# One weight tile of a mixture-of-experts layer moved into the memory of x and of work space: a blind prediction on one Trainium2 core

## The chip, the cores and the metric

One NeuronCore of one Trainium2 chip runs the whole program. Its engines are named as the profile names them: PE (TensorE, the matrix engine), PEld (its weight load), DVE (VectorE), ACT (ScalarE), POOL (GpSimd) and SP (SyncE, which issues nearly all transfers here; SPq is its queue). The metric is the device time of one execution in microseconds (us); less is better.

## The reference

Two transformer blocks follow each other on 256 tokens of width 1024, all in float32. The first is attention with eight heads, a layer norm and a mixture of experts; the second is a recurrent mixer with a short convolution, and a gated feed-forward net. What takes most of the time is the mixture of experts: 32 experts, each token goes to the four with the highest router logits.

```python
logits = (xt @ w_router + b_router)
top_logit, top_e = lax.top_k(logits, TOP_K)        # TOP_K = 4 of 32 experts
gate = jax.nn.softmax(top_logit, axis=-1)
...
h = xb @ w_gu[e] + b_gu[e]                          # [rows, 1024] @ [1024, 2048]
h_gate, h_up = jnp.split(h, 2, axis=-1)
h_gate = jnp.minimum(h_gate, SWIGLU_LIMIT)
h_up = jnp.clip(h_up, -SWIGLU_LIMIT, SWIGLU_LIMIT)
act = h_gate * jax.nn.sigmoid(SWIGLU_ALPHA * h_gate) * (h_up + 1.0)
return act @ w_down[e] + b_down[e]                  # [rows, 1024] @ [1024, 1024]
...
y = jax.ops.segment_sum(y_assign * gate, tok_sorted)
h = layer_norm(DEEPNORM_ALPHA * h + f, ln_g[i, 1], ln_b[i, 1])
```

## The kernel before

**Weight tiles.** All 32 experts are computed, so all their weights come in from HBM: per expert four gate and up tiles and two down tiles of 2 MB each (16 KB on each of 128 partitions). They are called gu*e*.*c* (c from 0 to 3) and dn*e*.*c* (c 0 or 1) in this text. The list `loads` holds them in the order of transfer: gu0.0 to gu0.3, gu1.0 to gu1.3, dn0.0, dn0.1, gu2.0 to gu2.3, dn1.0, dn1.1, gu3.0 and so on. Each is one `dma_start` on SP's queue (`load_run`, L125).

**Ten places.** During the mixture of experts a tile lies in one of ten places that are taken in rotation: six of the pool `wa`, open from the start, and four of the pool `wb` (`IN_B`), which is opened once the attention's memory is free. `weight(key, AHEAD)` asks for a tile and has `pump` queue the loads up to nine tiles further on; the load of the tile that is ten later in the list needs the place of the tile just used, so SP waits there until PE has read it. gu2.0 follows into the place of gu0.0, gu3.2 into that of dn0.0, dn2.0 into that of gu2.0.

**Order of the work.** For each expert `gate_up(e)` (L779, with the bias at L785) multiplies the gathered token rows by the four gate and up tiles, `swiglu` (L760 to L764) makes the activation on DVE and ACT, `transpose_act` (L794) turns it, and one expert later `finish(e - 1)` runs `down` (L807), `down_out` (L816) and, for odd experts, `combine` (L830, L831) into `y`. Two experts share one gathered batch: `make_batch` (L683) gathers it, `weigh_batch` (L748 to L755) prepares its weights. `y` is the memory of `xtok`, which held x for the attention. `start_y` fills `y`: eight multiplications and additions of rows on DVE (L655, L657) with the rows broadcast by PE (L259) through the two banks "m" of PSUM, a transpose and its copy `GT` (L661, L662), and four products with the down biases `bdn` (L667, L668). It is called after `gate_up(0)`. `bdn`, the output piece `ys`, the gate piece `sw_g` and the activation `at` are tiles of the pool `p2`; `bdn` and `ys` share a tag, each tag has one buffer.

Outside the stretches that are marked as ordered by hand, the framework orders the instructions of each engine itself when the program is built: among those that are ready by its own reckoning, the one that comes first in the program. After expert 15 a branch (`overflow`, L836) covers experts with more than 64 rows; here it is not taken.

Of the kernel before, what the change touches and what calls it, by code (L numbers as in the profile page):

```python
# [22 lines left out]
P = 128  # L23
# [60 lines left out]
def block_kernel(ctx: ExitStack, tc: tile.TileContext, a: dict, out: bass.AP, dbg=None):  # L84
# [37 lines left out]
    def load_run(t, w, r0, n):  # L122
# [3 lines left out]
                          .rearrange("(p k) c -> p (k c)", k=n))  # L126

    def load_run_last(t, w, r0, n):

        cols = w.shape[1]  # L130
        v = t[:, 0:n * cols].rearrange("p (k c) -> p k c", c=cols)
        for k, m in ((0, 2), (2, 1), (3, 1)):
            nc.sync.dma_start(v[:, k:k + m], w[r0:r0 + n * P, :]
                              .rearrange("(p k) c -> p k c", k=n)[:, k:k + m])
# [26 lines left out]
    for e in range(NE + 1):  # L161
        gu = [(("gu", e, c), load_run, (w_gu[e], c * 256, 2)) for c in range(4) if e < NE]
        dn = [(("dn", e - 1, c), load_run, (w_dn[e - 1], c * 512, 4)) for c in range(2) if e > 0]
        loads += dn + gu if e == OVF_AT else gu + dn
    end_moe = len(loads)
    loads[-1] = (loads[-1][0], load_run_last, loads[-1][2])
# [17 lines left out]
    def pump(upto):  # L184
        while state["next"] < min(upto, len(loads)):
            i = state["next"]
            key, fn, args = loads[i]
            slot = (i - first_moe) % (SLOTS_A + len(IN_B))
            if first_moe <= i < end_moe and slot in IN_B:
                if "b" not in pools:  # L190
# [8 lines left out]
    def weight(key, ahead=SLOTS_A - 1):  # L199
        pump(order[key] + 1 + ahead)  # L200
        return tiles.pop(key)
# [402 lines left out]
    with ExitStack() as c2:  # L604
# [6 lines left out]

        bdn = p2.tile([NE, D], F32, name="bdn", tag="ys")
        nc.gpsimd.dma_start(bdn, a["moe_b_down"][0])

# [143 lines left out]
        def swiglu(dst, pg, pu):  # L758
            gt = p2.tile([P, 512], F32, name="sw_g", tag="sw_g")
            V.tensor_scalar(gt, pg, LIMIT, None, op0=OP.min)  # L760
# [5 lines left out]
        def gate_up(e):  # L766
# [5 lines left out]
            for c in range(4):  # L772
                w = weight(("gu", e, c), AHEAD).rearrange("p (k c) -> p k c", c=2 * FF)
                for k in range(2):
                    kt = 2 * c + k
                    for q, dst in ((0, pg), (1, pu)):
                        for h in range(2):
                            c0 = q * FF + h * 512
                            mm(dst[h * CAP:(h + 1) * CAP, :], xs[:, kt, col:col + CAP],  # L779
                               w[:, k, c0:c0 + 512], start=(kt == 0), stop=(kt == KT - 1))  # L780
                if c == 0:
                    for q, dst in ((0, pg), (1, pu)):
                        for h in range(2):
                            c0 = q * FF + h * 512
                            mm(dst[h * CAP:(h + 1) * CAP, :], sel_e, bgu[:, c0:c0 + 512],  # L785
                               start=False, stop=False)
            at = p2.tile([P, 512], F32, name="at", tag="act")
            swiglu(at, pg, pu)
            return at

        def transpose_act(at, tag="aT", copy=nc.any.tensor_copy):
            pt = bank("atp", [P, 4, P], "t")
            for j in range(4):
                nc.tensor.transpose(pt[:, j, :], at[:, j::4], ident)  # L794
            aT = p2.tile([P, 4, P], F32, name="aT", tag=tag)
            copy(aT, pt)  # L796
# [13 lines left out]
        def down_out(e, pd):  # L810
            if e % 2 == 0:
                ys_pair[e // 2] = p2.tile([P, 2, 512], F32, name="ys", tag="ys")
            ys = ys_pair[e // 2]
# [19 lines left out]
        def overflow():  # L833

            n = nc.values_load(cnti[0:1, 0:1], min_val=0, max_val=NE)
            with tc.If(n > 0), tc.For_i(0, n, 1) as e:  # L836
                for g in range(2):
# [31 lines left out]
                    for kt in range(KT):  # L869
                        for q in range(2):  # L870
                            w = p2.tile([P, FF], F32, name="ow", tag="ys")
                            nc.sync.dma_start(
# [6 lines left out]
                    for h in range(2):  # L879
                        at = p2.tile([P, 512], F32, name="oat", tag="act")  # L880
                        swiglu(at, acc[0][h], acc[1][h])
# [3 lines left out]
                    for kt in range(KT):  # L885
                        w = p2.tile([P, D], F32, name="owd", tag="ys")
                        nc.sync.dma_start(w, w_dn[bass.ds(e, 1), kt // 4 * 512 + kt % 4:kt // 4 * 512 + 512:4, :]
# [55 lines left out]
        for e in range(NE):  # L943
# [11 lines left out]
            if e == NE - 1:  # L955
# [5 lines left out]
                break  # L961
            if e == 0:
                start_y()
            if e % NB == NB - 1 and e + 1 < NE and e + 1 != OVF_AT:
# [492 lines left out]
```

## Time and profile before

| | |
|---|---|
| Median of three runs | 1403.62 us (1400.08 to 1406.6) |
| The profiled execution | 1397.48 us |
| Its span, first to last instruction | 1395.7 us |
| PE busy | 1319.1 us, 95% |
| Read from HBM | 476.70 MB, 342 GB/s over the span |
| Granted clock of PE, mean | 0.991 |

The profiled execution is 1.78 us longer than its span and 6.1 us shorter than the median of the runs. A busy PE in this table is one with a matmul in its pipeline; the stretches below show which of PE and the transfers waits for the other.

### The profile page before, as it was taken

To read this page: it belongs to the slowest core of one execution; us is meant where nothing else is said; L and a number is where in the kernel's file an instruction comes from. 1 tells how busy PE (TensorE), PEld (TensorE's weight loads), DVE (VectorE), ACT (ScalarE), POOL (GpSimd) and SP (SyncE) were. 2 spreads that over 40 slices of the span, in tenths; PEclk is the share of its full clock that TensorE was granted. 3 is DMA by queue.
4 is the path that set the end of the run, shared out by engine and by line. 5 is a ranking of instruction groups with operands and counts; after the bars stand their busy time and mean duration, and the time that the engine had idled before them with its cause. 6 is when DMAs were issued, how large, how long until landed. Compare 5 with 4: busy or idle time off the path is not lost.

```text
span 1395.7 us, 16947 instructions
## 1 busy us (share of the span) xinstructions
PE 1319.1 (95%) x7162; PEld 749.0 (54%) x7162; DVE 527.6 (38%) x925; ACT 324.8 (23%) x571; POOL 73.2 (5%) x47
## 2 busy tenths in 40 slices
PE   9999999999999998798988989999899999999998
PEld 8887334334333332343433323333235998899997
DVE  4675322222222112221221212212115686777776
ACT  4553010011011000000001000000114445655554
POOL 2520000000000000000000000000003321000000
PEclk9999999999999999999999999999999999999999
DMA  8977999999999999989999999999999424555500
GB/s 260 356 284 295 381 426 427 427 426 427 428 426 426 427 427 427 424 350 428 427 428 425 428 426 426 427 427 428 427 421 387 148 81 161 184 199 190 182 1 31
DMA packets 74948, 478.91 MB, mean 343 GB/s; under 512 B 4764, under 2 KB 31972, under 8 KB 50196
## 3 DMA queue, kind: packets, MB, share of 16 engines
q1 hardware_dynamic: 74756, 477.61, 84.1%
q8 instruction: 58, 0.95, 0.3%
q0 software_dynamic: 112, 0.17, 0.0%
q14 instruction: 22, 0.18, 0.0%
HBM read 476.70 MB, written 1.06 MB: 342 GB/s over the span
## 4 chain that ended last, share of the span: by engine, by line
PE 30%; DMA 25%; DVE 2%; ACT 0%; issue 0%; SPq 0%; DVEq 0%; ACTq 0%
PE pu L266 9%; DMA wb<-in_moe_w_gate_up_dram 8%; DMA w<-in_moe_w_gate_up_dram 8%; DMA wb<-in_moe_w_down_dram 6%; PE pq L266 4%; DMA w<-in_moe_w_down_dram 3%; PE pg L779 2%; PE pu L779 2%; PE pd L807 2%; PE fa L270 1%; PE fa L272 1%; PE fa L271 1%; PE pgat L683 1%; PE px L1224 1%; PE pc L830 1%; PE mo L272 1%
## 5 line engine op out<-in xcount | busy, mean ns | idle before, releaser
L779 PE MATMUL pg<-w,xs 128*64 128x512 f32 x616 | 177.2, 599 | 12.5 <-DMA w<-in_moe_w_gate_up_dram 12.5
L779 PE MATMUL pu<-w,xs 128*64 128x512 f32 x616 | 178.2, 592 | 0.0
L760 DVE TENSOR_SCALAR sw_g<-pg 128x512 f32<-128x512 f32 x32 | 22.1, 691 | 401.4 <-PE pg L779 401.4
L807 PE MATMUL pd<-w,aT 128*64 128x512 f32 x624 | 142.6, 596 | 16.3 <-DMA w<-in_moe_w_down_dram 15.7
L761 ACT ACTIVATE at<-sw_g 128x512 f32<-128x512 f32 x32 | 20.2, 630 | 552.1 <-DVE sw_g L760 552.1
L779 PE MATMUL pg<-wb,xs 128*64 128x512 f32 x408 | 112.1, 602 | 10.0 <-DMA wb<-in_moe_w_gate_up_dram 10.0
L779 PE MATMUL pu<-wb,xs 128*64 128x512 f32 x408 | 110.9, 597 | 0.0
L807 PEld LDWEIGHTS pd<-w,aT 128*64 128x64 f32 x624 | 44.9, 137 | 102.2 <-issue 76.2
L993 ACT CAST hi<-w 128x1024 fp32r<-128x1024 f32 x75 | 78.4, 1048 | 86.3 <-PE pu L266 39.4
L779 PEld LDWEIGHTS pu<-w,xs 128*64 128x64 f32 x616 | 51.3, 137 | 86.7 <-issue 86.4
L779 PEld LDWEIGHTS pg<-w,xs 128*64 128x64 f32 x616 | 46.8, 136 | 94.8 <-issue 85.3
L807 PE MATMUL pd<-wb,aT 128*64 128x512 f32 x400 | 92.6, 606 | 4.9 <-DMA wb<-in_moe_w_down_dram 4.9
L816 DVE COPY ys<-pd 64x512 f32<-64x512 f32 x32 | 21.9, 684 | 187.4 <-PE pd L807 187.4
L994 DVE TENSOR_TENSOR lo<-w,hi 128x1024 fp32r<-128x1024 f32 x60 | 74.0, 1234 | 43.1 <-ACT hi L993 40.4
L994 POOL TENSOR_TENSOR lo<-w,hi 128x1024 fp32r<-128x1024 f32 x15 | 36.0, 2406 | 1005.7 <-DVE st L1091 938.6
L683 PEld LDWEIGHTS pgat<-oh,h 128*128 128x128 f32 x512 | 66.8, 208 | 23.5 <-issue 21.9
L683 PE MATMUL pgat<-oh,h 128*128 128x128 f32 x512 | 72.1, 299 | 6.8 <-DVE oh L677 6.4
L796 ACT COPY aT<-atp 128x512 f32<-128x512 f32 x32 | 18.7, 585 | 228.2 <-PE pd L807 183.3
L779 PEld LDWEIGHTS pu<-wb,xs 128*64 128x64 f32 x408 | 31.6, 138 | 58.1 <-issue 58.1
L779 PEld LDWEIGHTS pg<-wb,xs 128*64 128x64 f32 x408 | 29.3, 137 | 62.4 <-issue 54.4
L830 PE MATMUL pc<-ys,wT 128*128 128x512 f32 x120 | 57.2, 609 | 2.4 <-DVE ys L816 2.4
L807 PEld LDWEIGHTS pd<-wb,aT 128*64 128x64 f32 x400 | 27.6, 138 | 56.5 <-issue 47.7
(321 smaller groups left out, 1865.6 us busy)
## 6 DMA issues: line engine op xcount, KB each, us to landing
w<-in_moe_w_gate_up_dram SPq DMA_DIRECT2D x77, 2048.0 KB
wb<-in_moe_w_gate_up_dram SPq DMA_DIRECT2D x51, 2048.0 KB
w<-in_moe_w_down_dram SPq DMA_DIRECT2D x38, 2048.0 KB
wb<-in_moe_w_down_dram SPq DMA_DIRECT2D x25, 2048.0 KB
w<-in_ffn_w_up_dram SPq DMA_DIRECT2D x22, 1024.0 KB
w<-in_w_in_dram SPq DMA_DIRECT2D x6, 2048.0 KB
w<-in_a_w_in_dram SPq DMA_DIRECT2D x5, 2048.0 KB
w<-in_ffn_w_down_dram SPq DMA_DIRECT2D x5, 2048.0 KB
```

What stands on the lines that cost most here:

```text
L266: mm(psum_ap, lhs[:, kt, :], rhs[:, kt, :], start=(i == 0 and kt == kts[0]), stop=(i == len(pairs) - 1 and kt == kts[-1]))
L272: mm(psum_ap, ll, rh, start=False, stop=last)
L683: mm(pg[:, j, :], h1[:, tt, chan(kt)], batches[b][1][:, tt].rearrange("p e s -> p (e s)"), start=start, stop=stop)
L760: V.tensor_scalar(gt, pg, LIMIT, None, op0=OP.min)
L761: act(dst, gt, AF.Sigmoid, scale=SW_ALPHA)
L779: mm(dst[h * CAP:(h + 1) * CAP, :], xs[:, kt, col:col + CAP], w[:, k, c0:c0 + 512], start=(kt == 0), stop=(kt == KT - 1))
L796: copy(aT, pt)
L807: mm(pd[h][h * CAP:(h + 1) * CAP, :], lhs, w[:, k, h * 512:(h + 1) * 512], start=(c == 0 and k == 0), stop=(c == 1 and k == 3))
L816: (nc.scalar.copy if h else V.tensor_copy)(ys[o:o + CAP, h, :], pd[h][h * CAP:(h + 1) * CAP, :])
L830: mm(pc, lhs[:, tt * P:(tt + 1) * P], ys[:, h, :], start=True, stop=True)
L993: nc.scalar.copy(hi, piece)
L994: (nc.gpsimd if on_pool else V).tensor_sub(lo, piece, f32(hi))
```

## The change

gu0.3, the fourth tile that the first expert needs, is taken out of its place in `loads` and put behind gu2.0 as the eleventh load. It gets a place of its own that is used once: its rows with k = 0 go to the memory of `xtok`, those with k = 1 to a new tile `late` of 8 KB a partition in `p2`, by two transfers of 1 MB (`load_run_rows`). The other tiles keep the rotation of ten, from which gu0.3 is left out: gu1.0 takes the place that gu0.3 had, every tile up to gu2.0 moves up by one, gu2.1 follows into the place of gu0.0, and from dn1.0 on each load follows into the place of the same tile as before. `late` later serves as `sw_g`, `at` and `ys`, and as `bdn`; so `bdn` is loaded after `gate_up(0)` and `start_y` is called after `gate_up(1)`, as `y` is the memory of `xtok`.

```diff
@@ -125,6 +125,12 @@
         nc.sync.dma_start(t[:, 0:n * cols], w[r0:r0 + n * P, :]
                           .rearrange("(p k) c -> p (k c)", k=n))
 
+    def load_run_rows(t, w, r0, n):
+
+        for k in range(n):
+            nc.sync.dma_start(t[k], w[r0:r0 + n * P, :]
+                              .rearrange("(p k) c -> p k c", k=n)[:, k])
+
     def load_run_last(t, w, r0, n):
 
         cols = w.shape[1]
@@ -162,6 +168,10 @@
         gu = [(("gu", e, c), load_run, (w_gu[e], c * 256, 2)) for c in range(4) if e < NE]
         dn = [(("dn", e - 1, c), load_run, (w_dn[e - 1], c * 512, 4)) for c in range(2) if e > 0]
         loads += dn + gu if e == OVF_AT else gu + dn
+
+    ONCE = first_moe + SLOTS_A + len(IN_B)
+    key, _, args = loads.pop(first_moe + 3)
+    loads.insert(ONCE, (key, load_run_rows, args))
     end_moe = len(loads)
     loads[-1] = (loads[-1][0], load_run_last, loads[-1][2])
     W2_ORDER = (2, 1, 0, 3, 5, 6, 4)
@@ -185,8 +195,12 @@
         while state["next"] < min(upto, len(loads)):
             i = state["next"]
             key, fn, args = loads[i]
-            slot = (i - first_moe) % (SLOTS_A + len(IN_B))
-            if first_moe <= i < end_moe and slot in IN_B:
+            slot = (i - first_moe - (i > ONCE)) % (SLOTS_A + len(IN_B))
+            if i == ONCE:
+                if "once" not in pools:
+                    return
+                t = pools["once"]
+            elif first_moe <= i < end_moe and slot in IN_B:
                 if "b" not in pools:
                     return
                 t = pools["b"].tile([P, 4096], F32, name="wb", tag=f"w{IN_B.index(slot)}")
@@ -197,7 +211,9 @@
             state["next"] += 1
 
     def weight(key, ahead=SLOTS_A - 1):
-        pump(order[key] + 1 + ahead)
+        upto = order[key] + 1 + ahead
+        if order[key] != ONCE:
+            pump(upto + (order[key] < ONCE < upto))
         return tiles.pop(key)
 
     xtok = const.tile([P, NT, D], F32, name="xtok")
@@ -609,8 +625,13 @@
         def xs_tile(n, shape):
             return p2.tile([P] + shape, F32, name=n, tag="xs")
 
-        bdn = p2.tile([NE, D], F32, name="bdn", tag="ys")
-        nc.gpsimd.dma_start(bdn, a["moe_b_down"][0])
+
+        late = p2.tile([P, 2 * FF], F32, name="late")
+        late_sw, late_act = (late[:, i * 512:(i + 1) * 512] for i in range(2))
+        late_ys = late[:, FF:2 * FF]
+        pools["once"] = [xtok.rearrange("p n d -> p (n d)"), late]
+        pump(ONCE + 1)
+        bdn = late_ys[0:NE]
 
         def gates():
 
@@ -756,7 +777,7 @@
             batches[b] = [xs, wT]
 
         def swiglu(dst, pg, pu):
-            gt = p2.tile([P, 512], F32, name="sw_g", tag="sw_g")
+            gt = late_sw
             V.tensor_scalar(gt, pg, LIMIT, None, op0=OP.min)
             act(dst, gt, AF.Sigmoid, scale=SW_ALPHA)
             V.tensor_mul(gt, gt, dst)
@@ -770,21 +791,23 @@
             pu = bank("pu", [P, 512], "u")
             sel_e = selb[:, e:e + 1].to_broadcast([96, CAP])
             for c in range(4):
-                w = weight(("gu", e, c), AHEAD).rearrange("p (k c) -> p k c", c=2 * FF)
+                w = weight(("gu", e, c), AHEAD)
+                if (e, c) != (0, 3):
+                    w = [w[:, k * 2 * FF:(k + 1) * 2 * FF] for k in range(2)]
                 for k in range(2):
                     kt = 2 * c + k
                     for q, dst in ((0, pg), (1, pu)):
                         for h in range(2):
                             c0 = q * FF + h * 512
                             mm(dst[h * CAP:(h + 1) * CAP, :], xs[:, kt, col:col + CAP],
-                               w[:, k, c0:c0 + 512], start=(kt == 0), stop=(kt == KT - 1))
+                               w[k][:, c0:c0 + 512], start=(kt == 0), stop=(kt == KT - 1))
                 if c == 0:
                     for q, dst in ((0, pg), (1, pu)):
                         for h in range(2):
                             c0 = q * FF + h * 512
                             mm(dst[h * CAP:(h + 1) * CAP, :], sel_e, bgu[:, c0:c0 + 512],
                                start=False, stop=False)
-            at = p2.tile([P, 512], F32, name="at", tag="act")
+            at = late_act
             swiglu(at, pg, pu)
             return at
 
@@ -792,7 +815,10 @@
             pt = bank("atp", [P, 4, P], "t")
             for j in range(4):
                 nc.tensor.transpose(pt[:, j, :], at[:, j::4], ident)
-            aT = p2.tile([P, 4, P], F32, name="aT", tag=tag)
+            if tag == "sw_g":
+                aT = late_sw.rearrange("p (j s) -> p j s", s=P)
+            else:
+                aT = p2.tile([P, 4, P], F32, name="aT", tag=tag)
             copy(aT, pt)
             return aT
 
@@ -809,7 +835,7 @@
 
         def down_out(e, pd):
             if e % 2 == 0:
-                ys_pair[e // 2] = p2.tile([P, 2, 512], F32, name="ys", tag="ys")
+                ys_pair[e // 2] = late_ys.rearrange("p (h c) -> p h c", c=512)
             ys = ys_pair[e // 2]
             o = (e % 2) * CAP
             for h in range(2):
@@ -960,6 +986,8 @@
                 finish_all(prev[1], at)
                 break
             if e == 0:
+                nc.gpsimd.dma_start(bdn, a["moe_b_down"][0])
+            if e == 1:
                 start_y()
             if e % NB == NB - 1 and e + 1 < NE and e + 1 != OVF_AT:
                 make_batch(e // NB + 1)
...
```

Where a line with three dots stands, the same replacement of `p2` tiles by pieces of `late` in `overflow` is left out.

## Rows read from the trace of the kernel before

**Rows 1.** Busy time, granted clock, DMA share and GB/s by stretch.
```profile
core 0: us, PE busy (x) PEld busy (x) DVE busy (x) ACT busy (x) POOL busy (x), PEclk, DMA share, GB/s
...
300.00:400.00 100.00, 98.52 (x470) 38.33 (x468) 24.12 (x46) 10.19 (x20) 0.00 (x0) 1.00 1.01 426
...
700.00:800.00 100.00, 90.70 (x428) 35.69 (x426) 21.16 (x41) 7.88 (x16) 0.00 (x0) 1.00 1.01 427
```

**Rows 2.** Waits on SP's queue: 300 to 400 us (first row), 400 to 500 us (second).
```profile
SPq L125 <- PE pu L779: 62.3, 14, 8.0
...
SPq L125 <- DMA w<-in_moe_w_gate_up_dram: 31.8, 8, 4.5
```

**Rows 3.** The branch: timeline of SP's queue, and SP's waits from 600 to 625 us.
```profile
579.35 0.33 SPq L125 DMA_DIRECT2D wb<-in_moe_w_down_dram  x1
620.72 0.35 SPq L125 DMA_DIRECT2D w<-in_moe_w_gate_up_dram  x1
...
SPq L836 <- SPq L836: 39.8, 5, 20.1
```

**Rows 4.** The chain that ended last: the first of its DMA pieces, and what follows the last.
```profile
623.90 34.96 DMA w<-in_moe_w_gate_up_dram
...
1008.73 3.68 PE pd L807 x16
```

**Rows 5.** As rows 1, in stretches of 1 us and one of 4 us.
```profile
134.00:135.00 1.00, 1.00 (x9) 1.00 (x8) 0.47 (x2) 0.00 (x0) 0.00 (x0) 0.77 0.08 33
...
141.00:142.00 1.00, 1.00 (x8) 0.30 (x6) 0.00 (x0) 0.00 (x0) 0.00 (x0) 1.00 1.29 246
142.00:143.00 1.00, 1.00 (x6) 0.29 (x4) 0.00 (x0) 0.00 (x0) 0.00 (x0) 1.00 0.34 98
143.00:144.00 1.00, 1.00 (x8) 0.41 (x6) 0.00 (x0) 0.00 (x0) 0.00 (x0) 1.00 0.88 377
...
167.00:168.00 1.00, 1.00 (x6) 0.29 (x4) 0.00 (x0) 0.00 (x0) 0.00 (x0) 1.00 1.17 246
...
180.00:184.00 4.00, 4.00 (x20) 1.15 (x16) 0.00 (x0) 0.00 (x0) 0.00 (x0) 1.00 0.95 397
```

**Rows 6.** Timeline of SP's queue, the issues of weight tiles from 119 to 230 us.
```profile
119.92 0.80 SPq L125 DMA_DIRECT2D wb<-in_moe_w_down_dram  x2
140.63 11.06 SPq L125 DMA_DIRECT2D w<-in_moe_w_gate_up_dram  x4
...
166.16 0.33 SPq L125 DMA_DIRECT2D wb<-in_moe_w_down_dram  x1
...
180.81 0.33 SPq L125 DMA_DIRECT2D wb<-in_moe_w_gate_up_dram  x1
...
188.50 4.20 SPq L125 DMA_DIRECT2D w<-in_moe_w_down_dram  x2
...
227.08 3.76 SPq L125 DMA_DIRECT2D wb<-in_moe_w_gate_up_dram  x2
```

**Rows 7.** Timeline of POOL and DVE: when the places of gu0.3 are free.
```profile
119.24 0.51 POOL L613 DMA_DIRECT2D bdn<-in_moe_b_down_dram  x1 [41.71 <-PE ao L271]
...
119.90 0.69 DVE L489 SCALAR_TENSOR_TENSOR h<-xtok,ao 128x512 f32<-128x512 f32 x1 [1.29 <-PE ao L272]
```

**Rows 8.** Timeline of PE and DVE: start_y, and what PE does behind it.
```profile
151.26 0.61 PE L259 MATMUL lnr<-rows,selb 96*128 96x256 bf16 x4
...
160.39 3.88 PE L667 MATMUL pb<-bdn,GT 32*128 32x512 f32 x8
...
172.93 4.04 PE L683 MATMUL pgat<-oh,h 128*128 128x128 f32 x32
...
177.11 7.09 PE L807 MATMUL pd<-wb,aT 128*64 128x512 f32 x32
...
156.49 1.88 DVE L657 TENSOR_TENSOR xtok<-xtok,lnr 128x512 f32<-128x512 f32 x3
158.29 0.41 DVE L662 COPY GT<-gp 32x256 f32<-32x256 f32 x1
```

More of the change, by code (lines that the diff above doesn't have):

```diff
@@ L870, in overflow @@
                         for q in range(2):
-                            w = p2.tile([P, FF], F32, name="ow", tag="ys")
+                            w = late_ys
                             nc.sync.dma_start(
@@ L879, in overflow @@
                     for h in range(2):
-                        at = p2.tile([P, 512], F32, name="oat", tag="act")
+                        at = late_act
                         swiglu(at, acc[0][h], acc[1][h])
@@ L885, in overflow @@
                     for kt in range(KT):
-                        w = p2.tile([P, D], F32, name="owd", tag="ys")
+                        w = late_ys
                         nc.sync.dma_start(w, w_dn[bass.ds(e, 1), kt // 4 * 512 + kt % 4:kt // 4 * 512 + 512:4, :]
```

## The prediction, made before the changed kernel was run

> **What bounds the kernel now.** I read the stretches of the mixture of experts first. Between 300 and 400 us both sides look full: PE busy 98.5 of 100 us and the transfers at 426 GB/s; from 700 to 800 us the transfers are still at 427 GB/s, and PE has fallen to 90.7 [rows 1]. The reader is to see that the transfer rate is the constant and PE the one that gives way. At 427 GB/s a tile of 2.097 MB takes 4.91 us, and six tiles an expert take 29.5 us.
>
> Next I read what SP waits for. Up to 400 us it waits for PE to free a place (62.3 us in 100), then for earlier transfers to land [rows 2]. A wait for a place costs nothing while earlier tiles are still queued in front of the DMA engines; it costs as soon as that queue runs dry. So the question is when the queue last ran dry. In the fine stretches it did around 167 us (246 GB/s), and it came to its end once more around 182 us: 397 GB/s over 4 us is 0.28 us short of 427 [rows 5]. From then to the branch the rate is flat.
>
> The branch is the second gap. dn16.1 is issued at 579.35 us and the next tile at 620.72; in between SP waits 39.8 us in five waits at the branch's own line [rows 3]. I read these as waits until the queued tiles have landed, one after the other; so this gap comes after the last landing and moves with it. From 623.9 us the chain that ended last is DMA, piece behind piece, up to 1008.7 us, and then PE [rows 4]. Hence the end hangs on when the queue stops running dry near 182 us: a microsecond won there is won at the end, and one lost there is lost.
>
> **The change part by part.** *The eleventh tile.* The first ten tiles are issued by 120.7 us and moved by 134 us (33 GB/s in the next stretch); then the DMA engines stand nearly still until the place of gu0.0 is free, at 140.63 us [rows 5, 6]. gu0.3 as an eleventh tile fills 4.91 us of that. Its places are free in time: x is last read by DVE at 120.6 us, and the first tile of `p2`, which `late` becomes, could be loaded at 119.2 [rows 7]. It moves from about 134 to 139 us and is needed when PE has done three tiles of expert 0. gu2.0 is issued at 140.63 when the first tile is done, and four issues are 11.06 us apart [rows 6], so 3.6 us a tile: the need is at about 147.6 us. 9 us remain for it to land; no cost. That it comes as two transfers of 1 MB falls into the same gap.
>
> *What becomes of the 4.91 us.* They are a head start, not a saving. From dn1.0 on every tile follows into the place of the same tile as before, so its issue time is PE's, as before. The gain is the smallest spare time of any later issue: when it could start moving in the kernel before, minus when it is issued, minus the time from issue to movement. That time I take as 1.3 us. After the issue at 140.63 the first stretch has 246 GB/s, which at full rate puts the start at 141.4: 0.8 us, the lower end. The three stretches up to 144 us together moved 0.72 MB, 1.7 us of full rate, as if the start were at 142.3: 1.7 us, the upper end [rows 5, 6].
>
> With a queue that is just dry at 182.1 us, tiles start there and every 4.91 us after. gu3.2, into the place of dn0.0, is issued at 180.81: spare 182.1 - 180.81 - 1.3 = 0.0 us. dn2.0, two tiles later, into the place of gu2.0, is issued at 188.50: spare 182.1 + 9.8 - 188.5 - 1.3 = 2.1 us. gu5.0, ten tiles after gu3.2, is issued at 227.08: spare 182.1 + 49.1 - 227.08 - 1.3 = 2.8 us [rows 6]. Later ones have more, as PE needs less than 29.5 us for an expert. So if PE's order stayed as it is, the gain would be nothing; the slot of dn0.0 holds it up. dn1.1 at 166.16 us, where the queue was dry before, comes earlier by what start_y took ahead of it, but that alone helps nothing.
>
> *start_y behind gate_up(1).* Its work on PE is 0.61 us of broadcast rows and once more as much in two pieces, a short transpose, and 3.9 us of products [rows 8]: some 5.2 us, as each record overlaps the next a little. PE has no pause here, so moving it saves no PE time; it makes gate_up(1) end near 167.7 instead of 172.9 us. What changes is the cover. Eight row operations (three take 1.88 us, so 5.0 us), the copy GT of 0.41 us [rows 8] and the four operations of swiglu(1), of the same width (2.5 us), lie on DVE, and the products need GT and the rows. Before, PE ran gate_up(1) beside them. Now 8 us of DVE work stand between the end of gate_up(1) and the first product, about 176 us, and the gather waits behind the products for the same two banks. Ready for PE in that time is down(0), 7.1 us [rows 8]. If PE takes it there, dn0.0 is used up near 172 us instead of 180.8, and gu3.2 no longer limits; then the products, the gather (4.0 us) and gate_up(2) follow at 184.5 to 185.5 us, where pd ends at 184.2 us now and gate_up(2) follows. The gain is then dn2.0's 2.1 us less 0 to 0.7 us. That `bdn` is loaded later is covered by gate_up(1); `late` as one tile makes the same single buffers as the four tags did; the late `ys` waits for `bdn`'s last read, which is before it.
>
> Of the two orders, down(0) first (gain 1.4 to 2.1) and down(0) last without a pause (0), I take the first, as it is what PE can do while DVE works, and set -1.5 us. Ends: -2.1 and 0.
>
> **Scale.** The sum stands against the profiled execution: 1397.5 - 1.5 = 1396.0 us. That execution is 6.1 us under the median of the runs, and the runs themselves spread over 6.5 us. On the median's scale I forecast 1403.6 - 1.5 = 1402.1 us. About 0.5%, 7 us, is what a measurement of this kernel can tell from no change.
>
> **Rivals.** *The whole head start is kept* (0.13): 4.9 us, 1398.7 us. It needs gu2.0 done 2.8 us earlier than now, so that dn2.0's spare grows from 2.1 to 4.9: if PE did the 3.9 us of start_y's products only after the first tile of gate_up(2). Against it: they come first in the program and the gather waits behind them. The Trainium skill, Perfetto Trace Analysis, section Optimization Strategy, says to look for the gaps on the most-contended engine and make what blocks it start sooner; read plainly, filling 4.9 us of the DMA engines' gap at 134 us gives 4.9 us. The rows at 167 and 182 us speak against that reading: there the gap opens again, because of PE's pace.
>
> *PE stands still behind gate_up(1)* (0.14), slower: if the order keeps down(0) behind start_y and the gather, PE has 1.2 us of rows and transposes and then waits for DVE until 176 us, some 7 us. dn0.0 is then done at 180.8 + 7 = 187.8, and gu3.2 starts moving at 189.1 instead of 182.1: +7.0 us, 1410.6 us. It decides from the first 0.3 us of pause on, as gu3.2 has no spare. For it: DVE's 8 us are real, and the order is fixed when the program is built. Against it: down(0) needs nothing of start_y.
>
> *The change does nothing, or its order shifts by a little* (0.11): the slot of dn0.0 still limits, or the branch and the tail come out a microsecond or two otherwise: 1402 to 1405 us. That gu0.3 is late is part of it; it would have to be issued after some 135 us.
>
> **How the numbers follow.** My forecast with its bounds has 0.62. The likeliest cases alone, gain 0 to 2.1 us, with the spread of the runs (3 us either way), give 1399 to 1406 us. The range takes in the whole head start on a low median and the pause up to its price: 1395.5 to 1410 us. Faster by over 0.5% (under 1396.6) needs the whole head start and a low median: 0.06. Slower by over 0.5% (over 1410.6) is half of the pause and some of the order's mishaps: 0.09. The rest, 0.85, is no change that can be told.
>
> **What would show it.** Right: the stretch of 134 to 139 us at full rate with gu0.3's two transfers; gu3.2 issued near 172 us, dn2.0 near 188.5 to 189.5; DMA stretches under 427 GB/s between 181 and 190 us, where the head start is lost; the issue behind the branch and the last tile's landing earlier by 1 to 2 us. Wrong: a pause of PE before the first product of start_y, or gate_up(2) starting later than 186 us (the pause); the rate flat from 141 us on (the whole gain); a first expert that waits for gu0.3; or a gap at the branch of another length.

## The result and the profile after

The changed kernel takes 1409.34 us (median of 20 runs, 1404.24 to 1418.62), the kernel before 1404.12 us beside it (20 runs, 1393.77 to 1410.39): a ratio of 1.0054, 95% interval [1.0032, 1.0075]. It is slower, by 5 to 8 us (5.2 by the medians, 7.6 by the ratio). The prediction said 1402.1 us, a gain of 1.5, and gave slower by over 0.5% a chance of 0.09. That 1409.34 lies inside its range of 1395.5 to 1410 us is no merit of the forecast: the upper end was drawn up to the price of a rival, the pause of PE. The profiled execution after has a span of 1406.5 us (1395.7 before).

The first view is the timeline of SP's queue in the kernel after (start us, us, line, transfer).

```profile
123.34 0.38 SPq L131 DMA_DIRECT2D xtok<-in_moe_w_gate_up_dram  x1
123.77 1.35 SPq L131 DMA_DIRECT2D late<-in_moe_w_gate_up_dram  x1
...
142.06 4.20 SPq L125 DMA_DIRECT2D w<-in_moe_w_gate_up_dram  x2
...
192.21 3.76 SPq L125 DMA_DIRECT2D wb<-in_moe_w_gate_up_dram  x2
...
199.91 0.33 SPq L125 DMA_DIRECT2D wb<-in_moe_w_down_dram  x1
...
590.09 0.33 SPq L125 DMA_DIRECT2D w<-in_moe_w_down_dram  x1
631.40 0.35 SPq L125 DMA_DIRECT2D wb<-in_moe_w_gate_up_dram  x1
```

The two halves of gu0.3 go out at 123 us, as meant. The place of gu0.0 is free at 142.06 (140.63 before). But gu3.2, which I expected near 172 us, is issued at 192.21, 50.15 us after that first issue, where it was 40.18 us before [rows 6]. The last issue ahead of the branch comes 10.74 us later than before (590.09 and 579.35), and the gap behind it is what it was: 41.31 us here, 41.37 before [rows 3].

The timeline of PE shows why (in square brackets: the idle time before, and what ended it).

```profile
167.55 0.61 PE L275 MATMUL lnr<-rows,selb 96*128 96x256 bf16 x4
...
172.66 1.13 PE L817 MATMUL atp<-cmain,late 128*128 128x128 f32 x4 [4.49 <-DVE late L785]
...
175.55 7.19 PE L688 MATMUL pb<-late,GT 32*128 32x512 f32 x8 [1.34 <-DVE GT L683]
...
182.67 5.70 PE L704 MATMUL pgat<-oh,h 128*128 128x128 f32 x32
...
188.52 7.09 PE L833 MATMUL pd<-wb,aT 128*64 128x512 f32 x32
...
196.21 1.08 PE L802 MATMUL pg<-wb,xs 128*64 128x512 f32 x4
```

down(0), the row `pd`, stands behind start_y's products and the gather, and nothing is left for PE beside DVE: it waits 4.49 us for swiglu(0) and 1.34 us for GT, 5.83 us in all. Then the products take 7.19 us instead of 3.88 and the gather 5.70 instead of 4.04 [rows 8], 4.97 us more. Together 10.80 us, a little over the 9.97 by which gu3.2 is later after the first issue. Before, PE had no wait in this stretch: the profile lists none from 150 to 200 us.

The timeline of DVE in the same stretch says what PE waited for.

```profile
165.08 2.48 DVE L676 TENSOR_TENSOR xtok<-h,lnr 128x512 f32<-128x512 f32 x4 [25.31 <-PE pg L802]
167.47 0.68 DVE L781 TENSOR_SCALAR late<-pg 128x512 f32<-128x512 f32 x1
168.08 2.47 DVE L678 TENSOR_TENSOR xtok<-xtok,lnr 128x512 f32<-128x512 f32 x4
...
171.91 0.69 DVE L785 SCALAR_TENSOR_TENSOR late<-late 128x512 f32<-128x512 f32 x1
...
173.82 0.69 DVE L822 COPY aT<-atp 128x512 f32<-128x512 f32 x1 [0.49 <-PE atp L817]
...
175.09 0.40 DVE L683 COPY GT<-gp 32x256 f32<-32x256 f32 x1
```

start_y writes the memory of x, where half of gu0.3 now lies, so its eight row operations (L676, L678) follow gu0.3's products. These the built order puts behind all of gate_up(1), and so swiglu(0), swiglu(1) and start_y come to DVE at one time. down(0) needs swiglu(0) too: its turned activation `aT` is copied at 173.82 us (0.69 us long), so in this kernel it couldn't have filled the first wait, whatever its place in the order.

The bias `bdn` lies where the other half of gu0.3 lay, so its load is issued only behind gu0.3's products as well. POOL's timeline, and the row of that transfer (KB, us from issue to landing):

```profile
167.93 0.51 POOL L989 DMA_DIRECT2D late<-in_moe_b_down_dram  x1 [94.71 <-PE pu L802]
...
late<-in_moe_b_down_dram POOLq DMA_DIRECT2D x1, 128.0 KB, 7.1
```

It lands near 175.0 us, half a microsecond ahead of the first product.

Last, stretches of the kernel after (the granted clock is the third number from the end, then the DMA share and GB/s).

```profile
core 0: us, PE busy (x) PEld busy (x) DVE busy (x) ACT busy (x) POOL busy (x), PEclk, DMA share, GB/s
134.00:138.00 4.00, 4.00 (x27) 3.33 (x27) 2.87 (x16) 1.00 (x3) 0.00 (x0) 0.85 0.98 406
138.00:142.00 4.00, 4.00 (x20) 1.46 (x19) 1.03 (x6) 0.50 (x2) 0.00 (x0) 1.00 0.56 231
...
170.00:172.00 2.00, 0.00 (x0) 0.00 (x0) 1.93 (x4) 0.00 (x0) 0.00 (x0) 1.00 0.96 408
172.00:174.00 2.00, 1.34 (x6) 1.01 (x6) 1.47 (x3) 0.18 (x1) 0.00 (x0) 0.69 1.07 338
174.00:176.00 2.00, 0.66 (x2) 0.45 (x2) 2.00 (x4) 0.45 (x1) 0.00 (x0) 0.50 1.00 418
...
186.00:188.00 2.00, 2.00 (x18) 2.00 (x17) 1.37 (x4) 0.00 (x0) 0.00 (x0) 0.89 0.00 0
...
192.00:194.00 2.00, 2.00 (x12) 0.72 (x10) 0.00 (x0) 0.00 (x0) 0.00 (x0) 1.00 0.48 98
```

The gap of the DMA engines at 134 us is filled: 406 and 231 GB/s, where the kernel before moved 33 GB/s [rows 5]. It opens again and is wider: from 180 to 192 us nothing moves (0 GB/s). PE stands still from 168.2 to 172.7 us; from 172 us on the granted clock falls, to 0.50 from 174 to 186 us, the lower of its two levels (1.2 GHz), and this is where the products and the gather take longer.

### The profile page after: what moved, and what is told of

The parts are those of the page before. It is cut to its first block, busy times and chain, and to the rows that moved or that the text cites. A ratio compares the mean times of both kernels' runs of the same rounds, so it can differ in the third digit from the quotient of the medians.

```text
span 1406.5 us, 16935 instructions
## 1 busy us (share of the span) xinstructions
PE 1321.4 (94%) x7162; PEld 750.4 (53%) x7162; DVE 529.8 (38%) x926; ACT 324.6 (23%) x570; POOL 72.8 (5%) x47
## 4 chain that ended last, share of the span: by engine, by line
DMA 27%; PE 25%; DVE 2%; ACT 0%; issue 0%; SPq 0%; DVEq 0%; ACTq 0%
DMA w<-in_moe_w_gate_up_dram 14%; PE pu L282 9%; DMA w<-in_moe_w_down_dram 8%; PE pq L282 4%; DMA wb<-in_moe_w_down_dram 3%; DMA wb<-in_moe_w_gate_up_dram 3%; PE fa L286 1%; PE fa L287 1%; PE fa L288 1%; PE pd L833 1%; PE px L1252 1%; PE mo L287 1%; PE mo L288 1%; PE mo L286 1%; PE pg L802 1%; PE pv L1112 0%
## 5 line engine op out<-in xcount | busy, mean ns | idle before, releaser
L781 DVE TENSOR_SCALAR late<-pg 128x512 f32<-128x512 f32 x32 | 22.1, 692 | 390.3 <-PE pg L802 390.3
L833 PE MATMUL pd<-w,aT 128*64 128x512 f32 x608 | 138.0, 596 | 13.8 <-DMA w<-in_moe_w_down_dram 12.5
L782 ACT ACTIVATE late<-late 128x512 f32<-128x512 f32 x32 | 20.2, 630 | 551.4 <-DVE late L781 546.4
L833 PE MATMUL pd<-wb,aT 128*64 128x512 f32 x384 | 88.7, 605 | 6.7 <-DMA wb<-in_moe_w_down_dram 6.7
L842 DVE COPY late<-pd 64x512 f32<-64x512 f32 x32 | 21.9, 683 | 188.0 <-PE pd L833 188.0
L856 PE MATMUL pc<-late,wT 128*128 128x512 f32 x120 | 57.3, 610 | 2.4 <-DVE late L842 2.4
```

The costliest lines, as they stand in the source:

```text
L833: mm(pd[h][h * CAP:(h + 1) * CAP, :], lhs, w[:, k, h * 512:(h + 1) * 512], start=(c == 0 and k == 0), stop=(c == 1 and k == 3))
L842: (nc.scalar.copy if h else V.tensor_copy)(ys[o:o + CAP, h, :], pd[h][h * CAP:(h + 1) * CAP, :])
L856: mm(pc, lhs[:, tt * P:(tt + 1) * P], ys[:, h, :], start=True, stop=True)
```

## The experiments

One number separates the variants better than the time of a run does. *Start* is the first issue into the place of gu0.0, which comes when PE has used up the first tile of the experts; all that lies ahead of the experts is in it. From there I count to the issue of gu3.2 and to the last issue ahead of the branch, in the profiled execution of each kernel (issue times of SP's queue; the differences are mine).

| kernel | start | gu3.2 | last ahead of branch | start to gu3.2 | start to last | ratio of times [95%] |
|---|---|---|---|---|---|---|
| before | 140.63 | 180.81 | 579.35 | 40.18 | 438.72 | 1 |
| before_again | 143.01 | 184.83 | 582.80 | 41.82 | 439.79 | |
| split | 139.90 | 183.42 | 583.76 | 43.52 | 443.86 | 1.0015 [0.9989, 1.0041] |
| spread | 151.58 | 193.29 | 591.28 | 41.71 | 439.70 | 1.0017 [0.9992, 1.0042] |
| delay | 143.53 | 194.25 | 592.28 | 50.72 | 448.75 | 1.0030 [1.0006, 1.0054] |
| y_late | 151.49 | 201.52 | 599.51 | 50.03 | 448.02 | 1.0085 [1.0057, 1.0112] |
| after | 142.06 | 192.21 | 590.09 | 50.15 | 448.03 | 1.0054 [1.0032, 1.0075] |
| after_again | 140.44 | 191.54 | 589.48 | 51.10 | 449.04 | |
| hold | 142.33 | 191.96 | 589.92 | 49.63 | 447.59 | 1.0078 [1.0051, 1.0104] |
| warm | 143.64 | 192.34 | 590.11 | 48.70 | 446.47 | 1.0041 [1.0023, 1.0060] |
| b1 | 148.11 | 190.83 | 588.75 | 42.72 | 440.64 | 0.9996 [0.9969, 1.0023] |
| b2 | 144.26 | 182.63 | 584.08 | 38.37 | 439.82 | 1.0001 [0.9971, 1.0030] |
| b3 | 141.42 | 178.95 | 579.90 | 37.53 | 438.48 | 0.9958 [0.9931, 0.9985] |
| b3_again | 151.48 | 189.01 | 589.97 | 37.53 | 438.49 | 0.9995 [0.9968, 1.0021] |

Two things are read from it before any single run. In nine of the ten profiles where gu3.2 comes 41.7 us or more after the start, the last issue follows it by 397.8 to 398.0 us: from that place on the transfers alone set the pace, and each microsecond there arrives at the branch. The tenth is split, with 400.3 us: its transfers sag to 307 and 381 GB/s in the 4 us from 184 and from 188 us, after gu3.2 has been issued, and why is open. From the last issue to the end of the span it is 816.4 us before and after alike (813.5 to 816.6 over all fourteen profiles). And the start of one and the same kernel can differ by 10 us: b3 and b3_again have the same times from the start on, to 0.01 us, and 141.42 and 151.48 us ahead of it. A ratio of two medians holds that chance too: spread's 12 times lie in two groups, five at 1395.6 to 1400.2 us and seven at 1407.8 to 1410.7, and its profile, with a late start, is one of the seven.

**y_late**: the kernel before with start_y moved, and no eleventh tile.

```
-            if e == 0:
+            if e == 1:
                 start_y()
```

> The kernel before with start_y called after gate_up(1) and nothing else: gu0.3 keeps its place, ten places, bdn as before. Theory (the loss is the pause of PE, and the low clock behind it, that start_y leaves when no products of an expert are left to run beside its DVE work; down(0) stands behind it in the built order): PE pauses 4 to 6 us before start_y's products, they and the gather run at the lower clock level (7 and 5.7 us in place of 3.9 and 4.0), gu3.2 is issued some 8 to 11 us later after the place of gu0.0 is free than in the kernel before (40.2 us there), and the time is 8 to 11 us more, 0.6 to 0.8%. Rival (the eleventh tile itself costs, by its late arrival or its shared memory): no change, within 2 us.

The timeline of PE in y_late:

```profile
166.00 0.75 PE L794 MATMUL atp<-cmain,at 128*128 128x128 f32 x4
...
179.50 0.39 PE L259 MATMUL lnr<-rows,selb 96*128 96x256 bf16 x2 [1.54 <-DVE xtok L655]
...
181.90 0.39 PE L259 MATMUL lnr<-rows,selb 96*128 96x256 bf16 x2 [2.00 <-DVE xtok L655]
...
184.65 7.16 PE L667 MATMUL pb<-bdn,GT 32*128 32x512 f32 x8 [2.36 <-issue]
...
191.74 5.94 PE L683 MATMUL pgat<-oh,h 128*128 128x128 f32 x32
...
197.83 7.09 PE L807 MATMUL pd<-wb,aT 128*64 128x512 f32 x32
```

Three pauses, 5.90 us in all (the last, marked "issue", ends when DVE has copied GT, at 184.54 us), and again 7.16 and 5.94 us for the products and the gather. Here down(0) had its input early: expert 0's activation is turned (`atp`) at 166.00 us, and still `pd` comes at 197.83, behind the gather. PE takes it where the program has it. From the start to the last issue it takes 448.02 us, the kernel after 448.03 (449.04 in its second profile): the move alone makes the whole loss, and the eleventh tile gave nothing that is seen. The ratio is worse than after's; four of its six runs lie over 1414 us, six of after's 20 do, and its profile, one of the four, has a late start (151.49 us).

**hold**: the kernel after with gate_up(1) held behind the last product of gu0.3.

```
-            at = gate_up(e)
+            with (tc.issue_after(last[0].ins) if e == 1 else ExitStack()):
+                at = gate_up(e)
```

> The changed kernel with one edge more: PE takes all of gate_up(1) after the last product of gate_up(0), so gu0.3 is used where the first expert needs it. Theory (the built order put gu0.3 behind all of gate_up(1), which made the activation of expert 0 late, its four DVE operations and the turn of it fall into the pause): part of start_y's row operations move beside gate_up(1), the pause shrinks from 5.8 to about 3 us, the low clock behind it stays, gu3.2 comes 4 to 7 us sooner than in the changed kernel, and the time lies 3 to 6 us over the kernel before. Rival (gu0.3 has not landed when it is needed): PE waits for the transfer at gu0.3, some microseconds, and nothing is won on the changed kernel.

gu0.3's products now run from 150.1 to 153.7 us without waiting for their tile, so the tile is early enough. But start_y stays behind gate_up(1), as PE's timeline shows:

```profile
174.59 7.19 PE L688 MATMUL pb<-late,GT 32*128 32x512 f32 x8 [4.26 <-DVE GT L683]
```

It takes 49.63 us to gu3.2 instead of 50.15: the place of gu0.3's products in the order was worth half a microsecond, where I had expected 4 to 7 us; what costs is start_y behind gate_up(1).

**warm**: the kernel after with PE given products that nobody reads, where it stood still: 36 behind the first operation of swiglu(0) (n is 36 there), 10 in start_y behind GT.

```
+            if n:
+                junk = bank("junk", [P, 512], "t")
+                first = mm(junk[0:1, 0:T], ident[:, 0:1], gt[:, 0:T], start=True, stop=True)
+                with tc.issue_after(first.ins):
+                    warm(junk, n)
...
+            warm(bank("junk", [P, 512], "t"), 10)
```

> The changed kernel with 46 products that nobody reads: 36 behind the first operation of swiglu(0), where PE pauses, and 10 ahead of start_y's products. They add work and take none away. Theory (half of the loss is the lower clock level that follows the pause): the clock stays at 1.0, start_y's products take 3.9 in place of 7.2 us and the gather 4.0 in place of 5.7, gu3.2 comes about 5 us sooner than in the changed kernel, and the time is about 5 us less than the changed kernel's, 5 to 6 us over the kernel before. Rival (the products are slow since they wait for DVE or the transfers, not for the clock): they stay at 7 us, and the time is that of the changed kernel or more.

A row of PE's timeline in warm, and then stretches of it:

```profile
177.51 5.34 PE L689 MATMUL pb<-late,GT 32*128 32x512 f32 x8 [0.50 <-DMA late<-in_moe_b_down_dram]
```

```profile
176.00:180.00 4.00, 3.50 (x15) 1.50 (x13) 3.26 (x5) 0.22 (x1) 0.00 (x0) 0.97 0.99 419
180.00:184.00 4.00, 4.00 (x9) 1.83 (x8) 1.97 (x5) 0.00 (x0) 0.00 (x0) 0.50 0.21 90
184.00:188.00 4.00, 4.00 (x27) 4.00 (x26) 1.36 (x4) 0.00 (x0) 0.00 (x0) 0.68 0.00 0
```

The clock is kept through the wait for DVE, and falls all the same when start_y's products have begun (they start at 177.51 us and take 5.34, the gather 5.72). 1.45 us are won at gu3.2, little of the 4.97 us of the clock. The pause itself stays, as work that nobody needs doesn't shorten it: the products begin no sooner, and what they wait for last here is the load of the bias, issued at 169.51 us and landed 7.9 us later.

**split**: the kernel before with gu0.3 in two transfers of 1 MB, as the change loads it.

```
+    loads[first_moe + 3] = (loads[first_moe + 3][0], load_run_rows, loads[first_moe + 3][2])
```

> The kernel before with gu0.3 loaded by two transfers of 1 MB in place of one of 2 MB, into the same place at the same time; order and all else as before. Theory: no change, within 2 us, as the queue of transfers is long at that time. Rival (halved transfers cost, or shift the queue): 2 us more or above, and a later first product of expert 0.

The time is the same. What I had not expected stands in its stretches: with every engine in the order of the kernel before, the clock falls behind start_y's products, which take 4.48 us here.

```profile
158.00:162.00 4.00, 4.00 (x13) 1.24 (x10) 1.01 (x2) 0.48 (x1) 0.00 (x0) 1.00 1.03 438
162.00:166.00 4.00, 4.00 (x10) 0.99 (x10) 2.14 (x5) 0.00 (x0) 0.00 (x0) 0.60 0.98 418
166.00:170.00 4.00, 4.00 (x14) 1.14 (x12) 0.00 (x0) 0.00 (x0) 0.00 (x0) 0.55 0.41 90
```

**before_again, after_again**: both kernels unchanged, profiled once more, to see whether that fall belongs to an execution or to the order.

> The kernel before, unchanged, profiled a second time. In its first profile the granted clock stayed at 1.00 from 140 to 180 us, and the eight products of start_y took 3.88 us; in split, whose engines have the same order, the clock was 0.55 to 0.60 behind those products, and the place of dn0.0 came free 43.5 us after that of gu0.0 instead of 40.2. If the fall belongs to the order of the work and not to split's transfers, this execution shows it too: products of 4.2 to 4.6 us, one or two stretches of 4 us under 0.7, gu3.2 at 43 to 44 us, a span near 1399 to 1401 us. If split's transfers made it: clock 1.00, 40.2 us, a span near 1396.

> The kernel after, unchanged, profiled a second time. If the pause and the clock behind it belong to the order: pb at 7.1 to 7.2 us, pgat at 5.7 to 6.4 us, the clock at 0.50 over 8 us or more, gu3.2 49.5 to 50.5 us after the first issue into the place of gu0.0. If the fall of the clock was that execution's own: pb 3.9 us, pgat 4.0 us, gu3.2 at 45 to 46 us.

Stretches of before_again:

```profile
162.00:166.00 4.00, 4.00 (x11) 1.25 (x8) 1.55 (x3) 0.00 (x0) 0.00 (x0) 1.00 1.02 434
166.00:170.00 4.00, 4.00 (x12) 1.01 (x12) 1.60 (x4) 0.00 (x0) 0.00 (x0) 0.57 0.82 344
```

So the fall doesn't need split's transfers: it comes with the order of before, though not in each execution. The profile on which my sum stood was one without it, and this one has it, with products of 4.13 us and gu3.2 at 41.82 us instead of 40.18, less than I had expected (4.2 to 4.6, 43 to 44 us). After_again repeats after: the same waits of 4.49 and 1.34 us, products of 7.19, a gather of 6.64, 51.10 us.

**delay**: the kernel before with 64 unread products of one output row behind gate_up(1).

```
             at = gate_up(e)
+            if e == 1:
+                with tc.issue_after(last[0].ins):
+                    warm(bank("junk", [P, 512], "t"), 64)
```

> The kernel before with 64 products that nobody reads (bf16, 256 columns, one output row; 0.115 us apiece in the kernel warm, so 7.4 us) on PE between the last product of gate_up(1) and the gather of the next batch. PE does not stand still, no transfer is added, and start_y stays behind gate_up(0). The theory that a delay of PE at this place passes through the places of the weight tiles to the end: gu3.2 is issued some 47 to 48 us after the first issue into the place of gu0.0 (40.2 before, 50.2 after), the last expert tile lands 6 to 7.5 us later relative to that first issue, and the time is 7 us over the kernel before, a ratio of 1.0045 to 1.0055. The rival, that the transfers have slack there and it is the pause or the clock that costs: gu3.2 also late, but the last tile lands at most 2 us later and the ratio is under 1.002. A third outcome would be that the clock falls as well, behind the products of start_y or behind the added ones; then gu3.2 comes at 50 us or later.

They run from 179.17 us for 7.27 us. Stretches of delay:

```profile
166.00:170.00 4.00, 4.00 (x9) 1.06 (x10) 1.78 (x4) 0.00 (x0) 0.00 (x0) 0.56 0.95 401
...
178.00:182.00 4.00, 4.00 (x30) 2.28 (x28) 2.74 (x4) 0.63 (x1) 0.00 (x0) 1.00 1.00 393
182.00:186.00 4.00, 4.00 (x38) 3.01 (x37) 0.03 (x1) 0.00 (x0) 0.00 (x0) 1.00 1.00 424
```

The third outcome: the clock fell behind start_y's products (4.41 us), not behind the added ones. Counted from split, which had the fall too, gu3.2 is 7.20 us later and the last issue 4.89 us; from before_again 8.90 and 8.96 us. The added products are 7.27 us of the 8.90, the rest is a longer spell of the low clock. So against before_again the delay passes on whole; against split less arrives, as split's own way from gu3.2 to the last issue is 2.3 us longer. The ratio of 1.0030, some 4 us, is under the 7 that I expected; its interval reaches from 1.0006 to 1.0054, so some delay arrives in the time too.

**b1 and b2**: the order mended. b1 is hold with start_y's rows behind gate_up(0) again, and its GT and products (`start_products`, the second half of start_y) inside gate_up(1), behind the products of its third tile (the first lines). b2 also takes down(0) ahead of the gather, with `finish` ahead of `make_batch` (the last two).

```
+                if (e, c) == (1, 2):
+                    with tc.issue_after(last[0].ins):
+                        start_products()
...
+            if e == 1:
+                finish(*prev)
```

> The kernel after with three things in order: gu0.3's products are kept ahead of gate_up(1) as in hold, start_y's rows and their eight adds stand behind gate_up(0) again, and GT and the products of start_y behind gate_up(1)'s third tile, so that PE has work beside each piece of DVE's; the bias is loaded as soon as gu0.3 is used up. The theory that start_y's place behind gate_up(1), with nothing for PE to do beside it, costs the change its 10 us: no pause over 1 us between gate_up(1) and gate_up(2), gu3.2 issued 39.5 to 42 us after the first issue into gu0.0's place (50.2 after, 49.6 in hold), and the time within 3 us of the kernel before, a ratio of 0.998 to 1.002, some 7 us under the kernel after. The rival, that the eleventh tile or the places in late cost by themselves (a transfer that collides, the bias in the memory of gu0.3, the shared places): gu3.2 at 46 us or later and a ratio of 1.004 or more, though the order is mended.

> b1 with down(0) also put ahead of the gather for the next batch, so that the place of dn0.0 is free some 4 to 5 us sooner. My theory of spare times: gu3.2 is issued 34 to 37 us after the first issue into gu0.0's place, the queue of transfers then waits for dn2.0 (47.9 us after it before), and 1.4 to 2.1 us of the head start of 4.9 us are kept: a ratio of 0.9985 to 0.999, which five rounds may just not tell from 1. The rival that the whole head start is kept: 4.9 us, a ratio of 0.9965, and no stretch after 145 us under 400 GB/s. The rival that no tile's head start survives: the last expert tile lands as late relative to the first issue as in the kernel before, a ratio of 1.

PE waits for nothing between 164 and 200 us in b1, nor between 155 and 200 us in b2, and both take the time of the kernel before: 1400.98 and 1400.55 us beside 1400.82 (12, 12 and 29 runs). So the eleventh tile and the shared places by themselves cost nothing that these intervals (some 4 us either way) can tell, with start_y's rows in their old place. gu3.2 comes at 42.72 us in b1, a little over what I had expected, and at 38.37 in b2, over it too; in both the clock fell behind start_y's products (0.59 and 0.57 in the 4 us after them). Stretches of b2:

```profile
174.00:178.00 4.00, 4.00 (x12) 1.14 (x12) 1.02 (x3) 0.00 (x0) 0.00 (x0) 0.57 0.73 307
178.00:182.00 4.00, 4.00 (x20) 1.29 (x18) 2.77 (x4) 0.63 (x1) 0.00 (x0) 1.00 0.52 135
...
194.00:198.00 4.00, 4.00 (x24) 1.42 (x22) 0.00 (x0) 0.00 (x0) 0.00 (x0) 1.00 0.86 295
```

The queue runs dry a second time at 194 us: dn2.0, issued at 194.32, now limits, as I had said it would once gu3.2 did not. Of the 1.4 to 2.1 us that I expected b2 to keep nothing is seen: 439.82 us from the start to the last issue, against 438.72 and 439.79 in the two profiles of before.

**b3, b3_again and spread**: the four products of start_y one at a time between those of gate_up(1)'s last tile. b3 has it on b2, spread on the kernel before.

```
+                        mix = (e, c) == (1, 3)
+                        if mix:
+                            with tc.issue_after(last[0].ins):
+                                start_product(GT, 2 * k + q)
```

> b2 with the four products of start_y (eight records) spread over gate_up(1)'s last tile: one, then two of gate_up's, and so on, instead of all eight behind each other. In b1, b2, split and delay the granted clock was at 0.55 to 0.60 in the 4 us behind those products, and at 1.00 before. If a closed row of these products (32 rows of weights) is what precedes the fall, the clock stays over 0.9 through 170 to 190 us, gu3.2 comes 35 to 37 us after the first issue into gu0.0's place (38.4 in b2), dn2.0 at 47.5 to 48.5 (50.1), and the time is 1.5 to 2.5 us under b2's, a ratio of 0.998 to the kernel before. If what stands beside the products does not matter, the clock falls as in b2 and the ratio is b2's, 1.000.

> The kernel before with one thing of b3 alone: the four products of start_y spread over gate_up(1)'s last tile. No eleventh tile, no place in late, start_y's rows and the order of down(0) as before. It tells whose the 0.42% of b3 is. If it is the spreading (the clock): the clock over 0.9 from 160 to 190 us, gu3.2 at 40 to 42 us after the first issue into gu0.0's place (40.2 and 41.8 in the two profiles of before), and a ratio near 0.997, like b3's in this call. If it is the eleventh tile with down(0) ahead: a ratio of 0.999 to 1.001 here, and b3 again at 0.996. If b3's gain was chance: both within 0.998 to 1.002.

> b3 unchanged, beside spread and the kernel before on one chip: 0.996 as in the first call if the gain is its own, and 0.998 or more if it came from the chip of that call, whose runs of before had a median of 1404.2 us against 1400.8 in the call of b1 and b2.

Stretches of b3, and then of b3_again:

```profile
50.00:100.00 50.00, 48.95 (x320) 44.31 (x319) 36.00 (x46) 23.48 (x42) 25.60 (x7) 1.00 0.84 321
...
174.00:178.00 4.00, 4.00 (x20) 1.31 (x20) 3.06 (x7) 0.63 (x1) 0.00 (x0) 1.00 0.52 131
...
190.00:194.00 4.00, 4.00 (x24) 1.50 (x22) 0.00 (x0) 0.00 (x0) 0.00 (x0) 1.00 0.85 307
```

```profile
50.00:100.00 50.00, 41.77 (x258) 38.87 (x257) 28.07 (x20) 16.08 (x25) 20.90 (x7) 0.86 0.71 273
...
170.00:200.00 30.00, 30.00 (x136) 11.87 (x134) 9.94 (x22) 2.72 (x6) 0.00 (x0) 1.00 0.93 380
```

And one stretch of spread:

```profile
170.00:200.00 30.00, 29.50 (x138) 11.71 (x136) 9.34 (x21) 3.30 (x7) 0.00 (x0) 1.00 0.95 393
```

The clock stays at 1.00 from 160 to 190 us in all three profiles with spread products, and to 200 us in the two with a late start. It fell in six of the seven profiles where PE did the products in one piece and had not stood still for more than half a microsecond at a time before them (before_again, split, delay, warm, b1, b2; not in the first profile of before). The last issue comes 438.48 us after the start in b3 and 439.70 in spread, against 438.72, 439.79 and 443.86 in the three profiles with the order of before. b3 was 0.42% faster than before in its first set of runs and the same in the second, where its profile shows a late start (the clock is 0.86 from 50 to 100 us, in the attention). spread's 1.0017 beside it is the third outcome that I had named, a gain by chance. So I can't say that b3 beats the kernel before; it gives back what the change lost, with one microsecond or two to spare at most.

## Why the prediction was wrong

**What bounds the kernel: right.** The transfers run flat from the last dry queue on, the branch's gap moves with them (SP waits 39.8 us at its line, as before), and what is lost at gu3.2 is lost at the end. The row of SP's waits from 570 to 650 us after (us in total, times, longest):

```profile
SPq L862 <- SPq L862: 39.8, 6, 13.7
```

From the start to the last issue the profile of after is 9.31 us longer than the first profile of before, 8.24 us longer than the second and 4.17 us longer than split, which has before's order and some 2.4 us more behind gu3.2: the 5 to 8 us of the timed runs lie within, so no other cause is needed.

**The eleventh tile: right.** It fills the gap, costs nothing that is seen in b1 and b2, and would have been there in time, as hold showed. What is wrong beside it is "That `bdn` is loaded later is covered by gate_up(1)": the load began behind gate_up(1), and landed half a microsecond ahead of the products that need it.

**The step that failed** is the choice between two orders for down(0): "I take the first, as it is what PE can do while DVE works". The built order left down(0) behind the gather, where the program has it: make_batch stands ahead of finish. I had taken readiness for an order. y_late shows it bare, with the input of down(0) there at 166 us and down(0) run at 197.83. In the kernel after the readiness was missing as well: "down(0) needs nothing of start_y", but it needs swiglu(0), which came to DVE together with start_y's rows; so down(0) could not have begun before 174.5 us. So where I had set a gain of 1.5 us, PE waited 5.83 us and worked 4.97 us longer. When b2 moved the call, down(0) went ahead, and gu3.2 came 4.35 us sooner than in b1; the kernel after with that call alone moved was not run.

**The rival's size.** "PE stands still behind gate_up(1)", at 0.14 and +7.0 us, is what happened, with the sign that the prediction named for it, a pause of PE before start_y's first product. The pause measured 5.83 us. The rival left out two things. The clock fell with the pause, and 4.97 us more went into the products and the gather. And gu0.3's products, which I had in their old place, went behind gate_up(1), so that swiglu(0) joined the work that DVE had to do in that time; hold, without that, still paused 4.26 us. That its +7.0 us lies so near the 5 to 8 us of the timed runs is luck in part: in the profiles gu3.2 is 9.97 us later than in the execution that the sum stood on, and other executions of before have the fall of the clock that this one lacked.

**The sums of spare time: right in kind.** I gave gu3.2 no spare; 398.54 us from its issue to the last one in the first profile of before, against some 397.9 where it limits, make it 0.6 us. dn2.0 as the next limit was right: b2's and b3's queues run dry in front of it. In b3 it is issued 49.23 us after the start (190.65 us), against 47.87 before; of the 2.1 us of spare that leaves 0.7, and 0.24 us are seen. The whole head start of 4.91 us was kept by no variant. The Trainium skill (Perfetto Trace Analysis, Optimization Strategy) says to find the gaps on the most contended engine and to make what blocks it start sooner. b3 fills the gap with no wait of PE left, and it comes back at 174 us (131 GB/s) and 190 us (307 GB/s). So filling a gap gave a gain here only as far as what limits the issues behind it moved too.

**The scale.** I put the sum against one profiled execution, and named that it lay 6.1 us under the median, but not why. Part of it may be the clock behind start_y's products: 1.00 in that execution, 0.57 in the next, which takes 1.07 us more from the start to the last issue.

## What to carry to other kernels

A block that moves in the program takes its place in the built order along with all that stands behind it; before costing its move at nothing, look in the order for what the engine will do while the block waits. A delay on an engine off the bound reaches the end where it holds the place of the next transfer: list the issues with no spare, and check each of them. And when runs of one kernel spread over more than the effect, count from an event inside the program, as here from the first tile used to the last issue, and compare that.

## What the runs showed of the hardware

The granted clock can fall with PE full. In split PE is busy 4.00 of 4 us in each stretch from 158 to 174 us, and the clock goes to 0.60 and 0.55 behind eight records of products with 32 rows of weights, one behind the other; so it does in before_again, delay, warm, b1 and b2, and in the first profile of before it does not. With gate_up's products (128 rows) in between it stays at 1.00 (b3, b3_again, spread), and behind delay's 7.27 us of products with 128 rows and a single output row as well. The Trainium skill (TensorE: Matmul & The Clock Gate, What's actually happening) says that the gate follows how busy PE has been; by PE's busy time alone these rows disagree, and what sets the two kinds of products apart for the gate was not tried further. In the kernel after the fall begins with a pause of 4.49 us.

The start of the experts differs by 10 us between executions of one kernel (141.42 and 151.48 us in b3). These two ran on different chips, but the 12 runs of spread, all on one chip, fall in both groups too. The late ones have PE's clock at 0.86 to 0.90 and PE at 40 to 42 us of 50 busy between 50 and 100 us, in the attention. What makes an execution one or the other stays open.
